# A hybrid decoder step on one core: the loads of the prompt's attention tiles move from SyncE's DMA queue to GpSimd's, with new times of issue

## The chip, the cores and the metric

The kernel runs on one core of a Trainium2 chip. Its time is the device time of one launch in microseconds (us), the median over runs. Engines are called as in the profile: PE is TensorE's matmul side and PEld its weight load, DVE is VectorE, ACT is ScalarE, POOL is GpSimd, SP is SyncE, which here does nothing but issue transfers. A "queue" of SP, ACT or POOL is the row of instructions of that engine: it runs in order, so an instruction that waits holds up all behind it.

## The reference, cut to what matters

One step of a two-layer decoder, for a prompt of 2048 new tokens and for 8 sequences of 8 new tokens each that continue 4096 cached tokens. The first layer is a gated linear recurrence, the second an attention with 16 heads of 64 over keys and values made once (`shared_kv`), with a cumulated log-forget value added to the scores. Cut to its core:

```
def fox_block(q, k, v, cq, ck, q_pos, k_pos):        # per block of queries, per head
    s = einsum('bqhd,bkhd->bhqk', q, k) * HEAD_DIM ** -0.5
    s = s + cq - ck                                   # cumulated log forget of query and key
    p = softmax(where(k_pos <= q_pos, s, -inf))
    return einsum('bhqk,bkhd->bqhd', p, v)

# prompt:  run_group(x_prompt, zero state, no past)          2048 tokens, causal
# samples: run_group(x_sample, state, past = cache[page_table])   8 x (4096 + 8) keys, 32 pages of 128 rows each
```

All numbers are float32; large products split an operand into a high and a low part of the type fp32r.

## The kernel before, in words

The program is written out by Python loops in program order, and a scheduler then places each instruction on its engine's queue by its own model of time; dependences become semaphore waits. The stages follow one another: the recurrence for a first and a second part of the prompt, the projections to keys, values, queries and gates (`phase_b`), the prompt's attention (`attention`), and the output projection (`project`). Beside the projections and the attention runs a second stream, the decoding of the 8 sequences (`decode`): SP fetches pages of cached keys and values (`pages`, L1093, four transfers of 256 KB into one `raw` tile, four such tiles), DVE transposes the key pages (`ktr`), PE makes scores (`dS`) and outputs (`dO`, L1262). `Side.along` sets how many steps of the one stream stand between two steps of the other, by hand-set costs.

The prompt's attention walks 64 units: 16 heads, each with four blocks of 512 queries (`qc` 0 to 3; even heads go up, odd heads down). A unit has 4(qc+1) ticks, one for each 128 keys, 40 ticks a head. In one tick PE multiplies keys and queries in two products (L1592 low and high parts `ka`, `qa`; L1593 `kbt`, `qbt`), ACT takes the exponential from a PSUM bank into a tile `p` (L1601; six of them, and the first tick of a unit goes into `acc`), and two ticks after every fourth, PE multiplies the four `p` with the values (`ops`, L1612) and POOL adds each `p` into `acc` (L108, `acc<-acc,p`), for the softmax's sum. A tile `p` comes free when both have read it. Ahead of a unit, PE makes its scores once more in part (`sx`, L1431) and DVE takes maxima.

Five kinds of tiles are loaded from scratch tensors in HBM for this:

- `qa` (L1419, `load_low`, 128 rows of 2 KB), one a unit, four buffers
- `qbt` (L1413, `load_unit`, 64 rows of 2 KB), one a unit, six buffers (`NQ`)
- `ka` (L1406, `load_head`, 128 rows of 8 KB), one a head, two buffers
- `kbt` (L1399 and L1400, `load_keys`, 64 rows of 8 KB and 3 rows of log-forget sums), one a head, two buffers
- `vvt` (L1407, in `load_head`, 512 KB in pieces of 256 bytes), one a head, two buffers

Those of head 0 (and the first units) go through ACT's queue. From then on `queue[0]` is SP, where they stand among the pages. `paged()` pins a transfer behind the latest page transfer in SP's queue. `done[1]` counts the units whose `qbt` was loaded, `done[2]` those whose scores are finished, and `LEAD` (18 ticks) says how far the maxima run ahead. After the unit's last product, its rows are scaled by the sums: small transfers `sums`, `r` and larger `sgt`, `ogd` go through SP too, and POOL does one multiplication for each (`sgt<-sgt,oT`).

Of the kernel before, what the change touches and what calls it, by code (L numbers as in the profile page):

```python
# [20 lines left out]
P = 128  # L21
# [6 lines left out]
H = 16  # L28
# [20 lines left out]
LEAD = 18  # L49
# [10 lines left out]
NQ = 6  # L60
AFT = 14
# [20 lines left out]
def f(ap):  # L82

    return ap.bitcast(F32)
# [3 lines left out]
def tile_hawk_fox(  # L88
# [8 lines left out]
    V, A, G, T, S = nc.vector, nc.scalar, nc.gpsimd, nc.tensor, nc.sync  # L97
# [9 lines left out]
    def tt(eng, out, a, b, op):  # L107
        eng.tensor_tensor(out, a, b, op=op)  # L108
# [8 lines left out]
    def paged():  # L117

        return tc.issue_after(place["S"]) if "S" in place else ExitStack()

    def together(mms, after=(), beside=False):

        first = mms[0]().ins
        for d in after:
            tc.add_manual_dep(first, d.ins.name, SYNC)
        if beside:
            behind("T", first)
        with tc.high_priority(), tc.issue_after(first):
            for mm in mms[1:]:
                mm()  # L130
# [38 lines left out]
    def dt_(name, shape):  # L169
        return dram.tile(shape, F32, name=name, tag=name)  # L170
# [11 lines left out]
    v_d = dt_("vd", [SEQ, D])  # L182
# [1151 lines left out]
    def attention(es):  # L1334
# [10 lines left out]
        vvs = [pool.tile([P, 16, HD], F32, name=f"vvt{i}") for i in range(2)]  # L1345
# [37 lines left out]
        units = [(h, qc) for h in range(H) for qc in ((0, 1, 2, 3) if h % 2 == 0 else (3, 2, 1, 0))]  # L1383
# [5 lines left out]
        def halves(h):  # L1389
            return ((0, half), (half, SEQ)) if h == 0 else ((0, SEQ),)  # L1390


        queue = [A]

        def load_keys(h):
            kb = kbs[h % 2]
            loaded.add(h)
            for lo, hi in halves(h):
                queue[0].dma_start(f(kb[0:64, lo:hi]), kd_d[h * HD:(h + 1) * HD, 1, lo:hi])  # L1399
                queue[0].dma_start(f(kb[64:67, lo:hi]), nc_d[h, :, lo:hi])  # L1400

        def load_head(h):
            hr = slice(h * HD, (h + 1) * HD)
            ka = pool.tile([P, SEQ], F32R, name="ka", tag="ka", bufs=2)
            for lo, hi in halves(h):
                queue[0].dma_start(f(ka[:, lo:hi]), kd_d[h * HD:(h + 1) * HD, :, lo:hi].rearrange("d x t -> (d x) t"))  # L1406
            queue[0].dma_start(vvs[h % 2][:, :, :], v_d[:, hr].rearrange("(k p) d -> p k d", p=P))  # L1407
            heads[h] = ka

        def load_unit(u):  # L1410
            h, qc = units[u]
            assert u < done[2] + NQ
            queue[0].dma_start(f(qbs[u % NQ][0:64, :]), qd_d[h * HD:(h + 1) * HD, 0, qc * 512:(qc + 1) * 512])  # L1413

        def load_low(u):
            if u < len(units):
                h, qc = units[u]
                qa = qas[u] = pool.tile([P, 512], F32R, name="qa", tag="qa", bufs=4)
                queue[0].dma_start(f(qa[:, :]), qd_d[h * HD:(h + 1) * HD, :, qc * 512:(qc + 1) * 512].rearrange("d x t -> (d x) t"))  # L1419
# [36 lines left out]
        def finish(u, ops, acc):  # L1456
            h, qc = units[u]
            pr, h2 = divmod(h, 2)
            if u % 8 == 0:
                oTs_["sums"] = pool.tile([P, 32], F32, name="sums", tag="sums", bufs=2)  # L1460
            sums = oTs_["sums"]
            if h2 == 0:
                oTs_[qc] = pool.tile([P, 512], F32, name="oT", tag="oT", bufs=5)
            oT = oTs_[qc][h2 * HD:(h2 + 1) * HD, :].rearrange("d (a r c) -> d a r c", a=2, r=2)
            for r in range(2):
                A.copy(oT[:, :, r, :], ops[r * HD:(r + 1) * HD, :].rearrange("d (a c) -> d a c", a=2))
            accs.append((qc, acc))
            if len(accs) == 4 or h == H - 1:
                later.after(2, lambda todo=accs[:]: total(h2, sums, todo, h >= H - 2))
                accs.clear()  # L1470
            if u >= len(units) - 4:
                later.after(5, lambda oT=[oTs_[qc]]: norm(pr, sums, qc, 1, oT))
            elif u % 8 == 7:
                later.after(5, lambda oT=[oTs_[c] for c in range(4)]: norm(pr, sums, 0, 4, oT))
# [53 lines left out]
        nks = [(qc + 1) * 4 for _, qc in units]  # L1528
        start = [sum(nks[:u]) for u in range(len(units))]
        done = [0, 0, 0]  # L1530
# [17 lines left out]
        tick = 0  # L1548
# [1 line left out]
        load_head(0)  # L1550
        load_low(0)
        load_low(1)
        queue[0] = S
        for _ in range(3):
            later.tick()
            yield 300
# [4 lines left out]
        def scores_bank():  # L1561

            if dec_done:
                wide[0] += 1
                if wide[0] % 2:
                    return psum["dec"].tile([P, 512], F32, name="st", tag="do"[wide[0] // 2 % 2], bufs=1)
            return ps3.tile([P, 512], F32, name="st", tag="st", bufs=2)
# [3 lines left out]
        def loads():  # L1571
            while lows[0] < len(units):
                v = lows[0]
                if tick < (start[v - 2] if v < 4 else min(max(start[v - 2], start[v - 3] + AFT), start[v] - 3)):
                    break
                with paged():
                    load_low(v)
                lows[0] += 1
            h, k = divmod(tick, 40)
            if k == 16 and h + 1 < H:  # L1580
                with paged():
                    load_head(h + 1)

        for u, (h, qc) in enumerate(units):
            for k in range(nks[u]):
                loads()
                ka, kb = heads[h], kbs[h % 2]
                qa, qb = qas[u], qbs[u % NQ]
                lo = max(0, k - qc * 4) * P
                ks = slice(k * P, (k + 1) * P)  # L1590
                ps = scores_bank()
                place["T"] = T.matmul(ps[:, lo:], ka[:, ks], qa[:, lo:], start=True, stop=False).ins  # L1592
                T.matmul(ps[:, lo:], kb[:, ks], qb[:, lo:], start=False, stop=(k < qc * 4))  # L1593
                if k >= qc * 4:
                    T.matmul(ps[:, lo:lo + P], identB[:, :], causal[:, :], start=False, stop=True)
                done[2] = u + (k == nks[u] - 1)
                if k == 0:
                    p = acc = pool.tile([P, 512], F32, name="acc", tag="acc", bufs=NACC)
                else:
                    p = pool.tile([P, 512], F32, name="p", tag="p", bufs=NP)  # L1600
                pair.append((k, lo, p, A.activation(p[:, lo:], ps[:, lo:], AF.Exp)))  # L1601

                def product(u=u, h=h, todo=pair, acc=acc, last=(k == nks[u] - 1)):


                    nonlocal ops
                    if todo[0][0] == 0:
                        ops = ops2[:, u % 2 * 256:u % 2 * 256 + 256]

                    def mm(k, lo, p, r):  # L1610
                        a0 = (lo // P + 1 - r) // 2
                        return T.matmul(ops[r * HD:(r + 1) * HD, a0 * P:], vvs[h % 2][:, k, :],  # L1612
                                        p[:, :].rearrange("p (a r c) -> p a r c", a=2, r=2)[:, a0:, r, :],
                                        start=(k == 0), stop=(last and k == todo[-1][0] - 1 + r))

                    together([partial(mm, k, lo, p, r) for k, lo, p, _ in todo for r in range(2) if lo <= (2 + r) * P],
                             [todo[-1][3]])
                    for k, lo, p, _ in todo:
                        if k:
                            tt(a_l(), acc[:, lo:], acc[:, lo:], p[:, lo:], ALU.add)  # L1620
                    if last:
                        finish(u, ops, acc)

                if k % 4 == 3:
                    later.after(2, product)
                    pair = []
                before = done[0]
                advance(tick)
                tick += 1
                later.tick()  # L1630
                if k + sum(nks[u - u % 4:u]) == 0 and h + 1 < H:
                    load_keys(h + 1)
                yield 4.1 * (512 - lo) * 0.42 + (done[0] - before) * 213

    lent, dec_done = {}, []
# [153 lines left out]
    done = 9  # L1789
# [6 lines left out]
    done = max(done, 41)  # L1796
# [61 lines left out]
    psum["att"] = banks(att, "psa", 6)  # L1858
    cost = sum(4.1 * 0.42 * (512 - max(0, k - qc * 4) * P) + 213 for qc in range(4) for k in range(4 * qc + 4)) * H
    side.along(attention(att), ((16 - FIRST) * TURN - side.spent) / (cost * SPAN))  # L1860
    place.clear()
    side.upto(1e12)
# [38 lines left out]
```

## Time and profile before

| | |
|---|---|
| median of 3 runs | 3025.98 us (3022.0 to 3029.27) |
| the profiled execution | 3028.43 us; its span, from first to last instruction, 3026.4 us |
| mean granted TensorE clock | 0.969 |
| busy share of the span | PE 93%, PEld 74%, DVE 60%, ACT 42%, POOL 36% |
| prompt's attention | from about 1740 to 2825 us of the span |
| bytes | 653.79 MB, 216 GB/s over the span |

Busy shares are averages over stages with different limits. A PE that is shown busy need not be at its peak, since the ends of pipelined matmuls are modelled, and instructions that issue transfers are not counted as busy on any engine.

### The profile page before, as it was taken

To read this page: it belongs to the slowest core of one execution; us is meant where nothing else is said; L and a number is where in the kernel's file an instruction comes from. 1 tells how busy PE (TensorE), PEld (TensorE's weight loads), DVE (VectorE), ACT (ScalarE), POOL (GpSimd) and SP (SyncE) were. 2 spreads that over 40 slices of the span, in tenths; PEclk is the share of its full clock that TensorE was granted. 3 is DMA by queue.
4 is the path that set the end of the run, shared out by engine and by line. 5 is a ranking of instruction groups with operands and counts; after the bars stand their busy time and mean duration, and the time that the engine had idled before them with its cause. 6 is when DMAs were issued, how large, how long until landed. Compare 5 with 4: busy or idle time off the path is not lost.

```text
span 3026.4 us, 60467 instructions
## 1 busy us (share of the span) xinstructions
PE 2803.4 (93%) x21614; PEld 2252.1 (74%) x21614; DVE 1805.5 (60%) x4012; ACT 1269.9 (42%) x2874; POOL 1084.4 (36%) x1199
## 2 busy tenths in 40 slices
PE   6998999998997999999999699998998999999998
PEld 5997789988887997888889556665665666565687
DVE  6877455425427775676564466656776756655344
ACT  4665342222125665534333234444544444355321
POOL 1653201000002653100000245665575656659422
PEclk9999999999998999999999889999999999999999
DMA  4224546888863226699999968898899888874343
GB/s 123 79 88 133 171 126 191 256 263 281 278 216 91 89 88 194 209 313 338 332 346 326 279 209 243 248 282 255 250 291 287 267 251 265 260 247 122 98 145 110
DMA packets 479103, 653.79 MB, mean 216 GB/s; under 512 B 91291, under 2 KB 277020, under 8 KB 471525
## 3 DMA queue, kind: packets, MB, share of 16 engines
q1 hardware_dynamic: 475174, 644.26, 67.4%
q10 hardware_dynamic: 3340, 3.56, 0.4%
q8 instruction: 171, 2.80, 0.4%
q0 software_dynamic: 288, 2.10, 0.2%
q14 instruction: 130, 1.06, 0.1%
HBM read 514.22 MB, written 135.16 MB: 215 GB/s over the span
## 4 chain that ended last, share of the span: by engine, by line
PE 59%; DMA 16%; DVE 9%; ACT 6%; SPq 5%; issue 3%; POOL 1%; ACTq 0%; DVEq 0%; POOLq 0%
PE ops L1612 7%; PE st L1592 4%; PE y L383 4%; PE y L384 4%; PE y L385 4%; DMA raw<-in_cache_k_dram 4%; PE sx L1431 4%; PE dO L1262 3%; DMA raw<-in_cache_v_dram 3%; PE st L1593 3%; PE dS L1148 3%; PE kv L383 3%; PE kv L385 3%; PE kv L384 3%; SPq L1093 2%
## 5 line engine op out<-in xcount | busy, mean ns | idle before, releaser
L108 POOL TENSOR_TENSOR acc<-acc,p 128x512 f32<-128x512 f32 (+3 forms) x576 | 640.9, 1114 | 347.7 <-PE ops L1612 211.2
L1601 ACT ACTIVATE p<-st 128x512 f32<-128x512 f32 (+3 forms) x576 | 291.3, 525 | 400.1 <-PE st L1593 177.5
L1180 DVE STREAM_TRANSPOSE ktr<-raw 128x1024 f32<-128x1024 f32 x256 | 308.2, 1226 | 125.1 <-DMA raw<-in_cache_k_dram 116.5
L1433 DVE TENSOR_REDUCE mxs<-sx 128x1 f32<-128x512 f32 x384 | 255.0, 681 | 141.0 <-PE sx L1431 139.6
L383 PE MATMUL kv<-wh,xh 128*128 128x256 f32 (+3 forms) x1088 | 310.0, 288 | 6.4 <-ACT wh L427 4.7
L384 PE MATMUL kv<-wl,xh 128*128 128x256 f32 (+3 forms) x1088 | 309.3, 287 | 5.7 <-DVE wl L428 5.7
L385 PE MATMUL kv<-wh,xl 128*128 128x256 f32 (+3 forms) x1088 | 309.6, 286 | 2.7 <-DMA xl<-xld 2.7
L1592 PE MATMUL st<-qa,ka 128*128 128x512 f32 (+3 forms) x640 | 269.9, 422 | 13.3 <-ACT p L1601 7.5
L1612 PE MATMUL ops<-p,vvt 128*64 128x256 f32 (+1 forms) x2176 | 262.9, 369 | 1.0 <-ACT p L1601 0.7
L1431 PE MATMUL sx<-kbt,qbt 96*128 96x512 f32 (+3 forms) x640 | 229.2, 416 | 29.9 <-DMA qbt<-qd 24.2
L1113 POOL TENSOR_TENSOR qw<-qb,amask 128x128 f32<-128x128 f32 x64 | 29.1, 460 | 618.1 <-PE dS L1148 325.3
L428 DVE SCALAR_TENSOR_TENSOR wl<-wst,gv,wh 128x256 fp32r<-128x256 f32 (+1 forms) x384 | 169.4, 504 | 131.8 <-ACT wh L427 131.5
L427 ACT ACTIVATE wh<-wst,gv 128x256 fp32r<-128x256 f32 (+1 forms) x384 | 164.6, 499 | 190.2 <-DMA wst<-in_w_kv_dram 72.7
L1593 PE MATMUL st<-qbt,kbt 128*128 128x512 f32 (+3 forms) x640 | 236.9, 370 | 0.0
L383 PE MATMUL qg<-xh,wh 128*128 128x512 f32 (+2 forms) x640 | 229.4, 359 | 0.0
L384 PE MATMUL qg<-xl,wh 128*128 128x512 f32 (+2 forms) x640 | 228.2, 357 | 0.0
L385 PE MATMUL qg<-xh,wl 128*128 128x512 f32 (+2 forms) x640 | 227.5, 356 | 0.6 <-DVE wl L428 0.6
L1612 PEld LDWEIGHTS ops<-p,vvt 128*64 128x64 f32 x2176 | 161.5, 141 | 88.2 <-issue 19.8
L383 PEld LDWEIGHTS kv<-wh,xh 128*128 128x128 f32 (+1 forms) x1088 | 203.5, 188 | 13.2 <-ACT wh L427 6.8
L384 PEld LDWEIGHTS kv<-wl,xh 128*128 128x128 f32 (+1 forms) x1088 | 203.2, 188 | 10.1 <-DVE wl L428 6.9
L385 PEld LDWEIGHTS kv<-wh,xl 128*128 128x128 f32 (+1 forms) x1088 | 204.8, 188 | 7.0 <-issue 3.7
L1592 PEld LDWEIGHTS st<-qa,ka 128*128 128x128 f32 x640 | 123.7, 193 | 112.8 <-issue 54.4
(297 smaller groups left out, 6356.3 us busy)
## 6 DMA issues: line engine op xcount, KB each, us to landing
raw<-in_cache_k_dram SPq DMA_DIRECT2D x512, 256.0 KB
raw<-in_cache_v_dram SPq DMA_DIRECT2D x512, 256.0 KB
wst<-in_w_kv_dram SPq DMA_DIRECT2D x48, 512.0 KB
wst<-in_b_w_in_dram SPq DMA_DIRECT2D x48, 512.0 KB
xt<-in_x_prompt_dram SPq DMA_DIRECT2D x32, 512.0 KB
wst<-in_a_w_in_dram SPq DMA_DIRECT2D x64, 256.0 KB
out_dram<-kf SPq DMA_DIRECT2D x128, 128.0 KB
sc<-cd SPq DMA_DIRECT2D x16, 1024.0 KB
```

What stands on the lines that cost most here:

```text
L108: eng.tensor_tensor(out, a, b, op=op)
L383: T.matmul(ps, lh(k), rh(k), start=(k == 0), stop=False)
L384: T.matmul(ps, lh(k), rl(k), start=False, stop=False)
L385: T.matmul(ps, ll(k), rh(k), start=False, stop=(k == nk - 1))
L428: V.scalar_tensor_tensor(wl[:, k, :], st[:, k, :], gk, f(wh[:, k, :]), op0=ALU.mult, op1=ALU.subtract)
L1180: behind("V", V.transpose(t.kts[pp][:, n], raw[:, :, pp * 256:(pp + 1) * 256]).ins)
L1431: T.matmul(ps[:, :w], qb[0:96, j * P:(j + 1) * P], kb[0:96, ck * 512:ck * 512 + w], start=True, stop=True)
L1433: place["V"] = V.reduce_max(mx[:, j, ck:ck + 1], ps[:, :w], axis=AX.X).ins
L1592: place["T"] = T.matmul(ps[:, lo:], ka[:, ks], qa[:, lo:], start=True, stop=False).ins
L1593: T.matmul(ps[:, lo:], kb[:, ks], qb[:, lo:], start=False, stop=(k < qc * 4))
L1601: pair.append((k, lo, p, A.activation(p[:, lo:], ps[:, lo:], AF.Exp)))
L1612: return T.matmul(ops[r * HD:(r + 1) * HD, a0 * P:], vvs[h % 2][:, k, :], p[:, :].rearrange("p (a r c) -> p a r c", a=2, r=2)[:, a0:, r, : ...
```

## The change

The loads of `qa`, `qbt`, `ka` and `kbt` after the first head's go through POOL's queue and are no longer pinned to the pages; `vvt` stays in SP's queue, pinned to a page. The times of issue in program order are new: `load_low` two ticks after the start of the unit three before (at most four buffers are in use); `load_unit` by a loop of its own, as soon as a buffer is free and the unit starts within `LEAD + nks/2 + 7` ticks; `load_keys` for the next head at tick 3 of a head (it was tick 0, behind that tick's products) and `load_head` at tick 12 (it was 16). No arithmetic changes.

```
         def load_head(h): ...
-            queue[0].dma_start(vvs[h % 2][:, :, :], v_d[:, hr].rearrange("(k p) d -> p k d", p=P))
+            with paged() if h else ExitStack():
+                (S if h else queue[0]).dma_start(vvs[h % 2][:, :, :], v_d[:, hr].rearrange("(k p) d -> p k d", p=P))
...
-        queue[0] = S
+        queue[0] = G
...
         def loads():
             while lows[0] < len(units):
                 v = lows[0]
-                if tick < (start[v - 2] if v < 4 else min(max(start[v - 2], start[v - 3] + AFT), start[v] - 3)):
+                if tick < (start[v - 2] if v < 4 else start[v - 3] + 2):
                     break
-                with paged():
-                    load_low(v)
+                load_low(v)
                 lows[0] += 1
+            while done[1] < len(units) and done[1] < done[2] + NQ and tick >= start[done[1]] - LEAD - nks[done[1]] // 2 - 7:
+                load_unit(done[1])
+                done[1] += 1
             h, k = divmod(tick, 40)
-            if k == 16 and h + 1 < H:
-                with paged():
-                    load_head(h + 1)
+            if k == 3 and h + 1 < H:
+                load_keys(h + 1)
+            if k == 12 and h + 1 < H:
+                load_head(h + 1)
...
-                if k + sum(nks[u - u % 4:u]) == 0 and h + 1 < H:
-                    load_keys(h + 1)
```

Where the instructions come to stand is shown at three places. The line numbers behind the change are higher by one to four (`qa` L1420, `qbt` L1414, `vvt` L1408). First SP's queue between two pages, where the tiles of head 2 are loaded, before:

```order
L1093 DMA raw<-in_cache_k_dram 128x512
L1419 DMA qa<-qd 128x512
L1399 DMA kbt_19862<-kd 64x2048
L1400 DMA kbt_19862<-ncd 3x2048
L1406 DMA ka<-kd 128x2048
L1407 DMA vvt_19859<-vd 128x16x64
L1413 DMA qbt_19866<-qd 64x512
```

and the same place of SP's queue after the change:

```order
L1093 DMA raw<-in_cache_k_dram 128x512
L1408 DMA vvt_19859<-vd 128x16x64
L1086 TENSOR_LOAD pt_115
L1093 ISA
L1093 DMA raw<-in_cache_v_dram 128x512
```

Five of six loads between these two pages are gone from SP; `vvt` stays. Second, POOL's queue at the end of head 0's longest unit and the start of head 1's (`qw` and `gmx` belong to the decoding), before:

```order
L108 TENSOR_TENSOR acc<-acc,p 128x512 x2
L108 TENSOR_TENSOR acc<-acc,p 128x384
L1113 TENSOR_TENSOR qw<-qb,amask 128x128 x2
L108 TENSOR_TENSOR acc<-acc,p 128x256
L108 TENSOR_TENSOR acc<-acc,p 128x128
L1128 MEMSET gmx 128x8
L108 TENSOR_TENSOR acc<-acc,p 128x512 x12
```

and after, with the loads for head 2 and the units to come:

```order
L1113 TENSOR_TENSOR qw<-qb,amask 128x128
L1420 DMA qa<-qd 128x512
L1406 DMA ka<-kd 128x2048
L1399 DMA kbt_19862<-kd 64x2048
L1400 DMA kbt_19862<-ncd 3x2048
L1414 DMA qbt_19866<-qd 64x512
L108 TENSOR_TENSOR acc<-acc,p 128x128
L1128 MEMSET gmx 128x8
L108 TENSOR_TENSOR acc<-acc,p 128x512 x12
```

Five loads in a row stand between the unit's last two additions, ahead of twelve full additions. Third, POOL's queue at the last change of heads with loads (from head 13 to head 14), before:

```order
L108 TENSOR_TENSOR acc<-acc,p 128x128
L108 TENSOR_TENSOR acc<-acc,p 128x512 x4
L108 TENSOR_TENSOR acc<-acc,p 128x384
L108 TENSOR_TENSOR sgt<-sgt,oT 128x512
L108 TENSOR_TENSOR acc<-acc,p 128x256
```

and after:

```order
L108 TENSOR_TENSOR acc<-acc,p 128x128
L108 TENSOR_TENSOR acc<-acc,p 128x512 x2
L1420 DMA qa<-qd 128x512
L1414 DMA qbt_19863<-qd 64x512
L108 TENSOR_TENSOR acc<-acc,p 128x512
L1420 DMA qa<-qd 128x512
L1406 DMA ka<-kd 128x2048
L1399 DMA kbt_19870<-kd 64x2048
L1400 DMA kbt_19870<-ncd 3x2048
L1414 DMA qbt_19864<-qd 64x512
L108 TENSOR_TENSOR sgt<-sgt,oT 128x512
```

Seven loads stand among the additions here, and six more follow further on (`qa`, `qbt`, `qa`, `qbt`, `qa`, `qa`): 13 in all around and behind this change of heads. PE's queue holds the same instructions before and after, with the decoding's products beside the same units; only some `sx` stand a few ticks earlier or later.

## Prediction

> **What bounds the kernel now.** I read the page first, then the busy times by stretch, then who waited for whom on PE, ACT and SP within the prompt's attention, and last the timeline at single waits. The page's busy shares:
>
> ```profile
> span 3026.4 us, 60467 instructions
> PE 2803.4 (93%) x21614; PEld 2252.1 (74%) x21614; DVE 1805.5 (60%) x4012; ACT 1269.9 (42%) x2874; POOL 1084.4 (36%) x1199
> ```
>
> PE is the bound over the whole program, and POOL's 36% is an average that hides where its work lies. The change touches only the attention, so I split it where the decoding ends (the first row: its last page is fetched at 2702 us), and add the stretch in which the attention starts:
>
> ```profile
> L1093 SPq DMA_DIRECT2D raw<-in_cache_v_dram x316: 327/333/8803, 1780.4 to 2702.1; - x158
> ...
> core 0: us, PE busy (x) PEld busy (x) DVE busy (x) ACT busy (x) POOL busy (x), PEclk, DMA share, GB/s
> 1730.00:1758.00 28.00, 14.23 (x51) 7.87 (x51) 7.78 (x26) 3.17 (x10) 0.67 (x2) 0.50 0.79 211
> 1760.00:2720.00 960.00, 903.58 (x8240) 578.11 (x8239) 626.72 (x1328) 436.70 (x1080) 589.64 (x562) 0.97 0.84 259
> 2720.00:2820.00 100.00, 94.22 (x560) 58.44 (x558) 52.26 (x99) 57.99 (x121) 90.68 (x77) 1.00 0.38 109
> ```
>
> Of POOL's 1084 us, 590 + 91 lie in these two stretches. In the body (960 us, decoding beside it) PE is busy 94% and POOL 61%; 56 us of PE are idle, all that a better supply could win. In the tail (the last two heads, no decoding) POOL is busy 91%: there it is as near to the bound as PE. What PE's idle time in the body waited for, and ACT for POOL in both stretches (the second ACT row is the tail's):
>
> ```profile
> PE dO L1262 <- DMA raw<-in_cache_v_dram: 19.4, 13, 3.1
> PE rp L1505 <- DMA r<-rs: 11.3, 5, 4.2
> PE st L1592 <- ACT p L1601: 5.9, 17, 0.8
> ...
> ACT p L1601 <- PE st L1593: 177.4, 124, 6.0
> ...
> ACT p L1601 <- POOL acc L108: 16.6, 10, 3.5
> ...
> ACT p L1601 <- POOL acc L108: 21.5, 24, 2.0
> ```
>
> No row shows PE waiting for `qa`, `qbt`, `ka` or `kbt` in the body: the loads that move are in time already. What they may cost today is what stands behind them on SP. In the body ACT waits for POOL to free a `p` 10 times only; in the tail, a tenth as long, 24 times.
>
> **What leaves SP.** SP's queue in the body, waits of the prompt's loads:
>
> ```profile
> SPq L1413 <- PE st L1595: 20.7, 9, 5.3
> ...
> SPq L1399 <- PE sx L1431: 16.5, 2, 16.0
> ...
> SPq L1419 <- PE st L1595: 14.4, 3, 8.7
> SPq L1413 <- PE sx L1431: 13.7, 13, 6.1
> ```
>
> These 65 us hold back pages, and so do the transfers. One case:
>
> ```profile
> 1782.80 0.43 SPq L1406 DMA_DIRECT2D ka<-kd  x1
> 1783.27 0.43 SPq L1407 DMA_DIRECT2D vvt<-vd  x1
> 1784.33 8.18 SPq L1093 DMA_DIRECT2D raw<-in_cache_k_dram  x4
> ...
> 1793.60 1.92 SPq L1093 DMA_DIRECT2D raw<-in_cache_v_dram  x4
> ...
> 1800.79 1.07 PE L1262 MATMUL dO<-raw,sx 128*32 128x256 f32 x16 [2.18 <-DMA raw<-in_cache_v_dram]
> ```
>
> After `ka` (1 MB) and `vvt` (512 KB) the next four page issues take 8.18 us instead of about 2, and PE waits 2.18 us for a value page. But `vvt`, the one in small pieces, stays on SP, and the bytes stay the same. So I take about half of the 19.4 us as won, 10 us, and of the 11.3 us for `r` (a small transfer issued behind pages and loads, of which the pages stay) 3 us: **−13 us**. The bounds are 0 and −31 us.
>
> [...] No row here shows two queues side by side in the body. [...]
>
> **What POOL gets.** Counts and durations of the moved issues, and the only transfer that POOL issues before:
>
> ```profile
> L1419 SPq DMA_DIRECT2D qa<-qd x62: 319/430/7628, 1739.8 to 2772.4; - x62
> ...
> L1413 SPq DMA_DIRECT2D qbt<-qd x61: 444/464/6912, 1728.6 to 2736.5; - x61
> ...
> L1399 SPq DMA_DIRECT2D kbt<-kd x15: 444/473/1372, 1729.1 to 2720.8; - x15
> ...
> L1400 SPq DMA_DIRECT2D kbt<-ncd x15: 293/482/502, 1737.8 to 2721.5; - x15
> ...
> L1406 SPq DMA_DIRECT2D ka<-kd x15: 331/430/1694, 1782.8 to 2723.5; - x15
> ...
> L324 POOL DMA_INDIRECT lg<-in_cache_logf_dram,idx x2: 1058/1140/1223, 465.8 to 486.3; - x2
> ...
> 1696.80 1.81 POOL L1354 MEMSET kbt<- 64x2048 f32 x1 [0.33 <-DMA raw<-in_cache_k_dram]
> ```
>
> 62+61+15+15+15 = 168 issues. A plain transfer issued by POOL is in no row. The nearest is the indirect one, 1.06 to 1.22 us of POOL for 128 rows of 8 KB, the shape of `ka`. I take its 1.14 us for each; the ends are SP's median, 0.43 us, and, as the longest that POOL spends on a tile of this size, the clearing of `kbt`, 1.8 us. Behind each issue in POOL's queue stand additions into `acc`; for these waits ACT (a `p` comes free only when POOL has read it), and for ACT waits PE's next scores.
>
> Waits on POOL for a free buffer I cost at nothing: the issue stands among additions whose `p` was made some ticks after the last read of that buffer, so POOL gets there later than PE. If that cover is gone, SP's 65 us above are the price, now in front of the additions.
>
> *Tail.* Around and behind the last change of heads stand 13 issues: 13 × 1.14 = 15 us. POOL has 100 − 90.7 = 9.3 us of idle there; since part of it is forced by order (the start of a unit waits for its first product) I let half absorb: **+10 us** (bounds: 13 × 0.43 = 5.6 less 9.3, no loss; 13 × 1.8 = 23).
>
> *Body.* 155 × 1.14 = 177 us come to 590 of 960: POOL goes from 61% to 80%. Whether that costs is a question of crowding: five loads in a row are 5.7 us in front of a run of additions. I scale ACT's wait for POOL as in a queue, by busy over idle: from 0.61/0.39 = 1.6 to 0.80/0.20 = 4.0, so 16.6 us become 42, 25 more. How much of it reaches PE? Of the 16.6 us now, PE shows 5.9 us of waiting for `p`, a third; with PE already busy 94%, I take half: **+12 us** (bounds: at 0.43 us an issue 68%, 2.2/1.6 of 16.6, 6 more, a third of them 2; at 1.8 us 90%, 9 / 1.6 of 16.6 = 95, 78 more, all of them).
>
> **The start.** The first scores wait, while all loads of head 0 come through ACT's queue:
>
> ```profile
> PE sx L1431 <- DMA qbt<-qd: 24.2, 1, 24.2
> PE st L1592 <- DMA qa<-qd: 4.3, 1, 4.3
> ```
>
> The transfers are busy 79% in that stretch at 211 GB/s. POOL is free at 1730 us (0.67 us of work in 28) and would now issue `ka` of head 1 (1 MB) there, which SP issued at 1782.8. 1 MB at 211 GB/s is 5 us of the transfer engines; I let **+3 us** of it fall on head 0's loads, bounds −3 (SP's own loads gone from between the pages) and +5.
>
> **Sum.** −13 + 10 + 12 + 3 = +12 us. The profiled execution took 3028.43 us (span 3026.4), 2.4 above the median of 3025.98; 12 us on the median give **3038 us**. The bounds added up: −31 + 0 + 2 − 3 = −32, and 0 + 23 + 78 + 5 = +106. What is late next where the page wait goes: PE's next instruction there needs `p` from ACT, which is the wait that grows.
>
> **Rivals.**
>
> *Faster: the pages come free and POOL has room.* For: POOL is idle 39% of the body, ACT waits there ten times longer for PE's scores than for POOL (177.4 and 16.6 us), and the page wait shown above follows a `ka`. If an issue costs POOL no more than SP (0.43 us) and all waits for value pages and `r` go: −31 + 0 + 2 + 3 = −26, 3000 us; with two thirds of the waits, −21 + 2 + 2 = −17, 3009. It decides when an issue on POOL is below about 0.8 us. Against: the only row for such an issue says 1.06 or more, and `vvt` stays. 0.28, at about 3009 us.
>
> *No relief of transfers.* The wait for pages stays as it is since bytes, transfer engines and `vvt` stay: 0 + 10 + 12 + 3 = +25, 3051 us. Against it speaks that 8.18 us of issue followed `ka` and `vvt` together. [...] 0.14.
>
> *POOL becomes the bound.* If an issue holds POOL 1.8 us, or waits for buffers: body 155 × 1.8 = 279, 90% busy, half of 78 = +39; tail 23 − 5 = +18; +3, −13: +47, 3073 us. For: additions come in runs, in which POOL has no idle time as in the tail. Against: the clearing writes 64 partitions and an issue writes none. 0.13.
>
> *The change doesn't do what it says:* the loads get stuck behind additions and PE starts waiting for `qa` or `kbt`. They are issued ten ticks or more ahead of use, and 40 ticks take about 68 us (960 us for some 14 heads), so POOL would have to be 17 us behind. Five such waits of 3 us on the forecast: 3053 us. 0.03.
>
> **How the numbers follow.** The forecast has 0.42, with an own range of 3026 to 3056 us. Range for 8 in 10: from 3003 (most of the faster case) to 3078 (the bound case at its middle). A measurement of this kernel can tell 0.2%, 6 us, from no change. Faster by more: most of the 0.28 and the forecast's low edge, 0.29. Within: 0.14, from the forecast's lower part and weak gains. Slower: the rest of the forecast and the three slow rivals, 0.57.
>
> **What would show it.** In the changed kernel's profile: the duration of POOL's issues (right at 1.0 to 1.25 us); POOL busy, with issues, about 80% of the body; ACT's wait for POOL, 42 us in the body for 16.6; PE's wait for value pages about 10 us for 19.4; the last two heads 10 us longer. The forecast is wrong if issues cost POOL under 0.6 us, if ACT's wait for POOL does not grow, or if PE waits for `qa`, `qbt`, `ka` or `kbt`.

## The result, and the profile after

The changed kernel takes 3104.13 us (3095.34 to 3110.5), the kernel before, run beside it, 3024.66: a ratio of 1.0259 (95% interval 1.0225 to 1.0293), which is 78 us of 3025. The forecast was 3038 us, its range 3003 to 3078. The direction was right, the size far too small. One run of e10_gate (3550.91 us) and one of e18_pin (5326.34 us), far slower than their others, are left out of what follows. The profiled execution took 3095.34 us; its page begins:

```profile
span 3093.4 us, 60582 instructions
PE 2823.9 (91%) x21614; PEld 2257.0 (73%) x21614; DVE 1807.8 (58%) x4012; ACT 1271.0 (41%) x2874; POOL 1166.7 (38%) x1367
```

POOL has 82 us more, where 168 issues at the 1.14 us assumed make 192. (Other than is said ahead of the prediction, POOL's issues do count as busy: it has 1367 instructions for 1199, 168 more.) Busy times by stretch, cut where head 14's first exponential begins and where head 15's last ends, two rows of before and two of after (time, then PE, PEld, DVE, ACT and POOL busy, granted clock, DMA share, GB/s):

```profile
1757.00:2721.60 964.60, 908.18 (x8260) 581.52 (x8258) 630.76 (x1337) 439.09 (x1087) 591.16 (x563) 0.97 0.83 258
2721.60:2825.00 103.40, 96.81 (x577) 59.75 (x576) 52.23 (x96) 61.36 (x129) 93.93 (x79) 1.00 0.39 112
...
1758.00:2764.10 1006.10, 920.20 (x8253) 583.97 (x8253) 632.50 (x1331) 438.16 (x1082) 666.95 (x712) 0.95 0.81 246
2764.10:2895.00 130.90, 110.63 (x602) 66.39 (x601) 54.98 (x105) 62.80 (x134) 98.48 (x93) 0.90 0.32 90
```

The attention took 1068.0 us and now takes 1137.0; outside it 2 us came back, which leaves the 67 us between the spans. The body lost 41.5 us, the last two heads 27.5. In both PE's *busy* time grew too: 908.2 to 920.2 and 96.8 to 110.6, together 25.8 us, while the granted clock fell from 0.97 to 0.95 and from 1.00 to 0.90. Not all of this is slower products: 22 products of the output projection fall into the second stretch for 4 before, some 7 us. Over the whole program the same 21614 products take 2823.9 us for 2803.4, 20.5 us more. The other 43.2 us are PE idle time (56.4 to 85.9, and 6.6 to 20.3). What it waited for in the body (us in total, times, longest), and whom ACT and POOL waited for:

```profile
ACT p L1605 <- POOL acc L108: 42.1, 20, 11.1
POOL sgt L108 <- DMA sgt<-sgd: 41.4, 7, 13.8
POOL qa L1420 <- PE st L1597: 32.6, 2, 32.3
POOL qa L1420 <- PE st L1599: 32.3, 20, 9.9
...
DVE ktr L1180 <- DMA raw<-in_cache_k_dram: 25.5, 9, 6.8
...
PE st L1596 <- ACT p L1605: 19.9, 23, 9.2
...
PE rp L1506 <- DMA r<-rs: 14.3, 5, 7.9
...
PE sx L1432 <- DVE mxs L1436: 8.5, 3, 7.8
...
PE dS L1148 <- DVE ktr L1180: 7.9, 2, 7.5
...
PE dO L1262 <- DMA raw<-in_cache_v_dram: 7.0, 6, 2.1
```

POOL's wait of 32.3 us for `qa` is at the start, where POOL waited as long before (33.0 us, for the first value products). The last column is what is new. In the body of before no wait of PE lasted longer than 4.2 us (for `r`); now four different ones last 7.5 to 9.2 us. The longest, in the timeline (start, duration, engine, line, and in brackets the idle time before it and what ended it):

```profile
2618.65 0.43 SPq L1522 DMA_DIRECT2D sgt<-sgd  x1
2618.90 0.53 POOL L1414 DMA_DIRECT2D qbt<-qd  x1
...
2633.23 1.26 POOL L108 TENSOR_TENSOR sgt<-sgt,oT 128x512 f32<-128x512 f32 x1 [13.81 <-DMA sgt<-sgd]
2634.45 3.71 POOL L108 TENSOR_TENSOR acc<-acc,p 128x128 f32<-128x128 f32 x6
2634.93 0.60 ACT L1605 ACTIVATE p<-st 128x512 f32<-128x512 f32 x1 [11.05 <-POOL acc L108]
...
2635.58 0.80 PE L1596 MATMUL st<-qa,ka 128*128 128x512 f32 x1 [9.18 <-ACT p L1605]
```

SP asks for `sgt` at 2618.65; it lands 14.6 us later. POOL waits for it with six additions behind, so all six `p` are held, ACT stops, PE stops. At the same place of before, `sgt` was asked for at 2583.80, its multiplication ran at 2591.96 after a wait of 5.16, and no addition stood ready behind it. What the clock does around this wait (PE busy, granted clock, DMA share, GB/s):

```profile
2616.00:2624.00 8.00, 6.52 (x49) 1.00 1.06 368
2624.00:2628.00 4.00, 2.41 (x64) 1.00 0.99 226
2628.00:2632.00 4.00, 0.00 (x0) 0.62 0.79 218
2632.00:2640.00 8.00, 4.42 (x42) 0.50 0.03 6
2640.00:2644.00 4.00, 4.00 (x18) 0.67 0.90 277
```

The clock falls to 0.50 in the wait and is still there some 6 us after PE has work again: by windows of 1 us it is 0.50 from 2629 to 2642 us and 1.00 from 2643. This wait is so paid twice: a product of `st` (L1597, 128x512) takes 0.63 us behind it at 0.50, and took 0.39 ahead of it at 1.00. Shorter ones can be, too: in the kernel before, PE waited 2.08 us for a page up to 1924.24 us and 2.88 us for `r` up to 2481.61 us, and the clock stood at 0.50 from 1926 to 1928 and from 2482 to 2488 us. Its rows around them:

```profile
1920.00:1940.00 20.00, 17.45 (x217) 0.91 0.81 260
...
2480.00:2500.00 20.00, 18.39 (x103) 0.83 0.74 247
```

By windows of 2 us the attention of before has 12 stretches at a lowered clock, that of the changed kernel 18, the longest 22 us for 10.

In the last two heads the timeline shows another stop (ACT's casts of the output weights, L101, stand ahead of the exponentials):

```profile
2779.19 1.05 ACT L101 CAST woh<-wst 128x1024 fp32r<-128x1024 f32 x1 [10.25 <-DMA wst<-in_b_w_out_dram]
2780.14 0.59 ACT L1605 ACTIVATE acc<-st 128x512 f32<-128x512 f32 x1
...
2780.79 0.80 PE L1596 MATMUL st<-qa,ka 128*128 128x512 f32 x1 [6.50 <-ACT acc L1605]
```

`ka`, `kbt` and `qbt` left POOL at 2764.1 to 2765.7, in the middle of SP's loads of those weights. The price of an issue on POOL (by line: ns, least, median, most):

```profile
L1420 POOL DMA_DIRECT2D qa<-qd x62: 553/572/631, 1724.6 to 2841.0; - x62
L1414 POOL DMA_DIRECT2D qbt<-qd x61: 528/528/583, 1725.3 to 2801.6; - x61
L1406 POOL DMA_DIRECT2D ka<-kd x15: 541/541/577, 1728.0 to 2764.1; - x15
```

It is half of the 1.14 us assumed, from 128 KB (`qbt`, 0.528) to 1 MB (`ka`, 0.541). By the prediction's own list this price should have brought the faster case. So the price of an issue does not explain the loss.

### The profile page after: what moved, and what is told of

The parts are those of the page before. It is cut to its first block, busy times and chain, and to the rows that moved or that the text cites. A ratio compares the mean times of both kernels' runs of the same rounds, so it can differ in the third digit from the quotient of the medians.

```text
span 3093.4 us, 60582 instructions
## 1 busy us (share of the span) xinstructions
PE 2823.9 (91%) x21614; PEld 2257.0 (73%) x21614; DVE 1807.8 (58%) x4012; ACT 1271.0 (41%) x2874; POOL 1166.7 (38%) x1367
## 4 chain that ended last, share of the span: by engine, by line
PE 48%; DMA 19%; DVE 6%; SPq 4%; ACT 4%; issue 3%; POOL 1%; DVEq 0%; ACTq 0%; POOLq 0%
PE ops L1616 6%; DMA raw<-in_cache_k_dram 5%; PE st L1596 3%; PE sx L1432 3%; DMA raw<-in_cache_v_dram 3%; PE dO L1262 3%; PE y L383 3%; PE y L384 3%; PE y L385 3%; PE kv L383 3%; PE kv L385 3%; PE dS L1148 3%; PE kv L384 3%; PE st L1597 2%; SPq L1093 2%
## 5 line engine op out<-in xcount | busy, mean ns | idle before, releaser
L1596 PE MATMUL st<-qa,ka 128*128 128x512 f32 (+3 forms) x640 | 272.5, 426 | 41.7 <-ACT p L1605 20.3
L1597 PE MATMUL st<-qbt,kbt 128*128 128x512 f32 (+3 forms) x640 | 239.0, 373 | 0.0
L383 PEld LDWEIGHTS kv<-wh,xh 128*128 128x128 f32 (+1 forms) x1088 | 204.8, 189 | 12.4 <-ACT wh L427 6.3
```

What stands on the lines that cost most here:

```text
L383: T.matmul(ps, lh(k), rh(k), start=(k == 0), stop=False)
```

## Experiments

Ratios are to the kernel before, run beside each; 0.01 is 30 us. Three theories to begin with. *Two queues*: the bytes of POOL's queue share the transfer engines with SP's (in the body SP's packets take 65.1% of the 16 engines' time and POOL's 15.0%, where SP's took 82.8% before), so `sgt`, `r`, pages and weights land late. *New times*: the loads come in bunches and too early. *POOL's time*: issues, and waits for buffers, stand in front of additions.

**Times alone, queue alone.** e1_times changes one line of the changed kernel; e2_queue takes the kernel before with its times:

```
e1_times:  -  queue[0] = G      e2_queue:  -  queue[0] = S
           +  queue[0] = S                 +  queue[0] = G      (loads unpinned; vvt on S, pinned)
```

> The changed kernel with its new times of issue, but the moved loads in SyncE's queue again (not pinned to a page). Theory 'two queues' (POOL's transfers run beside SP's and share the transfer engines with them, so that sgt, the last weights and pages land late): the loss goes, 3015 to 3045 us. Theory 'new times' (the loads come in bunches and too early): the loss stays, 3085 to 3115 us. Theory 'POOL's time' (155 issues of 0.55 us in front of additions): 3015 to 3045 us as well.

> The kernel before with its old times of issue, but the loads of qa, qbt, ka and kbt in GpSimd's queue, unpinned, and vvt on SyncE pinned, as in the change. 'Two queues': 3080 to 3120 us, as the changed kernel. 'New times': 3015 to 3045 us. 'POOL's time': 3080 to 3120 us.

e1_times: 1.0025 (1.0002 to 1.0047). e2_queue: 1.0243 (1.0222 to 1.0264). The new times cost some 8 us; the queue makes the loss, with the old times as well. *New times* falls.

**The late `sgt`.** e4_sgtV lets VectorE multiply, e10_gate puts five ticks more between the request for it and its use, e16_gate_before makes the same edit to the kernel before:

```
e4_sgtV:   -  tt(G, sg, sg, oT[qc - q0], ALU.mult)     +  tt(V, sg, sg, oT[qc - q0], ALU.mult)
e10_gate, e16_gate_before:
           -  later.after(3, gate)                     +  later.after(8 if n == 4 else 3, gate)
           -  (AFT + 7) * (qc // 2)                    +  (AFT + 12) * (qc // 2)
```

> The changed kernel with the multiplication sgt<-sgt,oT on VectorE in place of GpSimd, so that POOL no longer waits for the transfer of sgt in front of its additions (41 us of waits in 7 places in the changed kernel, up to 13.8 us, of which 9 us each reached PE twice). Theory 'POOL held by a late transfer': 20 to 40 us come back, 3065 to 3085 us. If the stall only moves to VectorE, which then holds maxima and transposes: 3095 to 3115 us. 'POOL's time': at most 10 us come back.

> The changed kernel with five ticks (about 8 us) more between the fetch of sgt and its use, and between the two pairs of fetches, for all but the last heads; nothing else moves. If sgt landing late (41 us of waits in 7 places) starts the stalls at the changes of even heads: 15 to 40 us come back, 3065 to 3090 us. If it only shares the crowding with its neighbours (r, key pages): 3090 to 3112 us.

> The kernel before with five ticks more between the fetch of sgt and its use, and between the two pairs of fetches (the edit of e10_gate). Its waits for sgt are 27.5 us on POOL in 8 places, at most 7.4 us, and PE waits 11.5 us for r. If POOL's wait reaches PE only when it is longer than the six tiles p cover, nothing is won: 3018 to 3032 us. If waits of any length cost, 10 us or more are won: 3005 to 3016 us.

e4_sgtV: 1.0235 (1.0213 to 1.0257), nearly the whole loss. In its waits in the attention (us in total, times, longest), DVE now stands for `sgt`, and PE 28.1 us for DVE's maxima (1.3 in the same row of before):

```profile
DVE sgt L108 <- DMA sgt<-sgd: 45.5, 9, 10.6
PE sx L1432 <- DVE mxs L1434: 28.1, 18, 6.8
```

e10_gate: 1.0189 (1.0144 to 1.0234); about 20 us came back. The late `sgt` is a part, not the root. e16_gate_before: 1.0062 (1.004 to 1.0083), slower, a miss of both expectations: PE's wait for value pages rose from 19.4 to 27.2 us. So the five ticks are no gain in themselves.

**The last two heads.** e11_tail goes back to SP's queue from tick 30 of head 13:

```
 def loads():
+    queue[0] = G if tick < 40 * 13 + 30 else S
```

> The changed kernel with GpSimd's queue until tick 30 of head 13, and SyncE's queue from there on. It asks for the last two heads, which took 131 us (from the first exponential of head 14 to the last of head 15) for 103.5 before. If POOL's transfers of that stage hold up the last weights' (ACT waited 10.3 us for them): the stage takes 103 to 112 us, the kernel 3078 to 3090 us. If the stage is late for another reason: 122 us or more, 3095 to 3112 us.

1.0153 (1.0118 to 1.0188), 3074.01 us. Its last two heads in the busy times by stretch:

```profile
2765.80:2870.20 104.40, 98.84 (x583) 61.09 (x582) 53.05 (x101) 62.68 (x133) 93.62 (x80) 0.98 0.39 113
```

104.4 us for 130.9, at a clock of 0.98, with the body as slow as before this edit (1004.7). So POOL's loads from there on cost this stage some 27 us, and the whole kernel 30.

**Issues alone.** e3_issue adds 168 transfers of 64 bytes to POOL in the kernel before; e13_pinned adds 163, each queued behind the latest addition:

```
e3_issue:    +  G.dma_start(tiny[r:r + 1, c * 16:c * 16 + 16], kd_d[0:1, 0, 0:16])
e13_pinned:  +  with tc.issue_after(place["G"]):
             +      G.dma_start(tiny[r:r + 1, c * 16:c * 16 + 16], kd_d[0:1, 0, 0:16])
```

> The kernel before with 168 transfers of 64 bytes added to GpSimd's queue at the changed kernel's places, which nobody reads; the loads themselves stay with SyncE. It asks what the issues alone cost POOL and the kernel. 'POOL's time': 92 us more on POOL, the kernel 30 us or more slower, 3055 us up. 'Two queues' and 'new times': 64 bytes take no bandwidth and wait for no buffer, so 0 to +12 us, 3020 to 3038 us.

> The kernel before with about 160 transfers of 64 bytes added to GpSimd's queue at the changed kernel's times, which nobody reads, each now queued behind the latest addition into acc so that none is pulled ahead. The loads stay with SyncE. If the issues alone (0.5 us each, 80 us of POOL) make the loss: 3070 us or more. If they have room in POOL's idle time: 3020 to 3045 us.

e3_issue: 1.0291 (1.0254 to 1.0328). It does not test what it should: nothing held the transfers at their places, and all 168 were issued before head 1 had begun, up to thirteen at a time. From its timeline of POOL:

```profile
1842.67 5.78 POOL L1575 DMA_DIRECT2D tiny<-kd  x12
1848.47 1.69 POOL L108 TENSOR_TENSOR acc<-acc,p 128x128 f32<-128x128 f32 x2
1850.10 1.96 POOL L1575 DMA_DIRECT2D tiny<-kd  x4
```

The three longer units of head 0 lost 81 us there. e13_pinned: 1.0058 (1.004 to 1.0077), some 18 us, for 82.8 us of POOL. Its group of issues (count, busy us, mean ns, idle time) and its busy times by stretch, body and last two heads:

```profile
L1576 POOL DMA_DIRECT2D tiny<-kd x163 | 82.8, 511 | 2.7 <-issue 2.7
...
1752.00:2708.60 956.60, 899.32 (x8255) 577.28 (x8255) 632.47 (x1336) 438.23 (x1087) 662.31 (x713) 0.97 0.84 261
2708.60:2824.30 115.70, 101.48 (x578) 61.15 (x577) 49.92 (x96) 60.59 (x129) 96.95 (x92) 0.96 0.35 105
```

This execution took 3027.92 us, the fastest of seven, 15 us under their median. In it the body lost nothing with POOL at 662 us (the changed kernel: 667), and the last two heads 12 us. ACT did wait longer for POOL than before, though never as long at once as in the changed kernel (whole attention; before, e13_pinned, changed kernel):

```profile
ACT p L1601 <- POOL acc L108: 38.1, 34, 3.5
...
ACT p L1617 <- POOL acc L1636: 56.0, 44, 5.2
...
ACT p L1605 <- POOL acc L108: 67.6, 46, 11.1
```

Little of it reached PE, whose wait for `p` in the scores was 7.5, 11.5 and 20.3 us.

**Half of the loads; another queue.** e7_q leaves `qa`, `qbt` on POOL, e8_k `ka`, `kbt`; e6_act sends all through ScalarE's queue:

```
e7_q:    ka, kbt:  +  (S if queue[0] is G else queue[0]).dma_start(...)
e8_k:    qa, qbt:  +  (S if queue[0] is G else queue[0]).dma_start(...)
e6_act:            -  queue[0] = G       +  queue[0] = A
```

> The changed kernel with only qa and qbt (123 issues, 24 MB, rows of 2 KB) in GpSimd's queue; ka, kbt go through SyncE's, unpinned. 'POOL's time': three quarters of the issues and all waits for buffers stay, so 3085 to 3105 us. 'Two queues' by bytes: half the loss, 3055 to 3080 us; if it is the 1.5 MB burst at each change of heads in rows of 8 KB that delays sgt: nearly no loss, 3030 to 3050 us.

> The other half: only ka and kbt (45 issues, 24 MB, rows of 8 KB, 1.5 MB at once per head) in GpSimd's queue; qa, qbt go through SyncE's, unpinned. 'POOL's time': a quarter of the issues, 3035 to 3055 us. 'Two queues' by bytes: half the loss, 3055 to 3080 us; if it is the burst in rows of 8 KB: nearly the whole loss, 3080 to 3105 us.

> The changed kernel with the moved loads in ScalarE's queue: a queue beside SP's still, but no instruction on POOL. 'Two queues': the loss stays, 3080 to 3120 us. 'POOL's time': it goes, 3015 to 3050 us (168 issues of about 0.45 us on ACT, which is busy 45% of this stage, and some waits for buffers in ACT's queue).

e7_q: 1.0061 (1.0038 to 1.0085). e8_k: 1.0082 (1.0057 to 1.0107). They add up to some 43 us, all loads cost 78: neither *POOL's time*, which put three quarters on `qa` and `qbt`, nor an even split by bytes. e6_act: 1.019 (1.0163 to 1.0218). It says little: ACT's own queue now stops ahead of exponentials, and PE waits 61.7 us for `p` in its value products. Its waits in the attention:

```profile
PE ops L1616 <- ACT p L1605: 61.7, 25, 9.4
ACT p L1605 <- DMA rawn<-ksd: 19.9, 2, 10.6
ACT p L1605 <- DMA raw<-in_cache_k_dram: 17.8, 5, 6.5
```

**Loads cut between the queues.** e5_row lets POOL fetch the first row of each load and SP the others; e9_rows16 does so with 16 rows (one of the three of log-forget sums); e12_spfirst exchanges the two queues:

```
+  G.dma_start(to[:n], src[:n])      # e5_row: n = 1; e9_rows16: n = 16
+  S.dma_start(to[n:], src[n:])      # e12_spfirst: S first, G the rest
```

> The changed kernel with every moved load cut in two: GpSimd's queue fetches only its first row (2 or 8 KB), SyncE's queue all other rows, unpinned. POOL so keeps every issue at its place with the same waits for buffers, and the bytes go back to SP's queue. Theory 'two queues' (it is the bytes beside SP's queue that make sgt, weights and pages late): 3025 to 3055 us. Theory 'POOL's time' (92 us of issues and 65 us of waits for buffers in front of additions): 3085 to 3115 us.

> The run with a row cut off again, now in sixteenths: GpSimd's queue fetches the first 16 rows of each moved load (of the log-forget sums, one of three), SyncE's queue the rest, so that no transfer has 127 rows. POOL keeps every issue at its place with its waits for buffers; 75 to 88% of the bytes, and the waits for buffers too, are in SP's queue again. 'POOL's time': 3085 to 3115 us. 'Two queues' (bytes beside SP's queue) and 'SP not held' (nothing in SP's queue waits for PE's scores any more, pages run ahead and sgt stands behind a longer backlog): 3030 to 3060 us.

> The same cut the other way: SyncE's queue fetches the first 16 rows of each moved load, GpSimd's the rest. SP's queue is held by the same waits for buffers again, but most bytes still run beside it. 'Two queues' by bytes: 3080 to 3115 us. 'SP not held': 3030 to 3060 us. 'POOL's time': 3085 to 3115 us.

e5_row: 1.3423 (1.3391 to 1.3455), no answer: the transfers of 127 or 63 rows hold up SP's queue. There an issue of `qbt` (63 rows) lasts 3.63 us in the median and up to 40.5, for 0.46 in the kernel before, one of `kbt` (63 rows) 5.25 for 0.47, and one of `qa` (127 rows) up to 39.6 us. From 1757 to 2900 us all transfers together moved 130 GB/s, and PE waited up to 62.4 us for a page. From its waits:

```profile
PE dO L1262 <- DMA raw<-in_cache_v_dram: 394.8, 20, 62.4
```

Why such issues last so long, no run shows. e9_rows16: 1.0288 (1.0243 to 1.0333), the whole loss, with most bytes in SP's queue again. e12_spfirst: 1.0379 (1.0339 to 1.0418), slower than any theory expected. Both double the number of transfers. They speak against *two queues*, and against the idea that SP's queue only has to be held by PE again.

**Bytes or queue.** e14_few_pool cuts the loads after the first heads' to 16 rows (the others keep older contents), with POOL's order kept (its waits for `qa` behind the start are 22.5 us for 32.5); e15_few_sync does the same through SP:

```
+  n = to.shape[0] if full else min(16, to.shape[0])
+  queue[0].dma_start(to[:n], src[:n])       # e14_few_pool: G, e15_few_sync: S
```

> The changed kernel with each moved load cut to its first 16 rows (all rows for the first two heads' keys and the first units' queries; the other rows keep older contents, so the attention is computed from partly stale keys and queries). POOL keeps every issue at its place with its waits; some 40 of 50 MB are not moved at all. If POOL's issues and waits make the loss: 3075 us or more, far above the control e15_few_sync. If the bytes beside SP's queue make it: near the control, within 20 us.

> The control of e14_few_pool: the same few rows with the same times of issue, through SyncE's queue (the attention computed from partly stale keys and queries as there). 40 MB less at about 260 GB/s leave the transfer engines some 150 us more idle: 2995 to 3035 us by every theory.

e14_few_pool: 1.0107 (1.0073 to 1.0142), 3058.73 us. e15_few_sync: 0.9937 (0.9915 to 0.9959), 3006.79. The first misses both expectations: it is under 3075 us, and not near its control. So POOL's queue costs 52 us over SP's with few bytes, and 71 with all (3104.13 less e1_times' 3033.31). If the parts add up, that leaves some 19 us for the bytes beside SP's queue, with an uncertainty nearly as large (the intervals of the four times are 7 to 11 us to either side). *Two queues* falls as the main cause.

**The place on POOL.** 163 issues cost 18 us, 168 loads with few bytes 52. In e13_pinned each stands behind an addition; in the changed kernel the scheduler places the loads, and behind the start 12 times four or five stand in a row. e18_pin pins all moved loads, e20_pin_qa `qa` alone:

```
+  with tc.issue_after(place["G"]) if queue[0] is G and "G" in place else ExitStack():
+      queue[0].dma_start(to, src)           # place["G"]: the latest addition into acc
```

> The changed kernel with each moved load queued on POOL behind the latest addition into acc at its time of issue (as the loads stood pinned behind pages before). Same queue, same bytes, same count of issues. If the loss is the place of the loads on POOL (pulled ahead, in rows, waiting for buffers with additions behind them: 67 us of such waits from the start of the attention): they become rare and 25 to 50 us come back, 3050 to 3080 us. If it is the bytes beside SP's queue, or the issues: 3090 to 3115 us.

> The changed kernel with only qa queued on POOL behind the latest addition; qbt, ka and kbt stay where the scheduler puts them, ten times four in a row in front of additions. If POOL's waits for qa's buffer (32 us behind the start, in 21 places, up to 9.9 us), with a row of loads and additions behind them, make the part that e18_pin took back: 3050 to 3072 us. If the rows themselves make it: 3085 to 3110 us.

e18_pin: 1.0094 (1.0063 to 1.0125), 3056.39 us: 48 us came back with the same queue, bytes and count. At the last change of heads, where seven loads stood around one addition, POOL's queue now reads:

```
L1397 DMA qa<-qd 128x512
L1397 DMA kbt_19870<-kd 64x2048
L1397 DMA kbt_19870<-ncd 3x2048
L1628 TENSOR_TENSOR acc<-acc,p 128x256
L1628 TENSOR_TENSOR acc<-acc,p 128x512
L1628 TENSOR_TENSOR acc<-acc,p 128x128
L1397 DMA qa<-qd 128x512
L1628 TENSOR_TENSOR acc<-acc,p 128x512 x2
L1397 DMA ka<-kd 128x2048
L1628 TENSOR_TENSOR acc<-acc,p 128x512
```

Behind the start no row is longer than three, and at one load only, a `ka`, does POOL wait (1.9 us, for ACT). Its body and last two heads by stretch, and its only wait of a load on POOL:

```profile
1760.00:2739.90 979.90, 913.30 (x8255) 584.03 (x8253) 633.25 (x1330) 438.11 (x1081) 671.06 (x713) 0.96 0.83 254
2739.90:2856.30 116.40, 105.84 (x597) 63.80 (x598) 50.14 (x104) 61.72 (x133) 98.51 (x95) 0.97 0.34 101
...
POOL ka L1397 <- ACT p L1609: 1.9, 1, 1.9
```

e20_pin_qa: 1.0137 (1.0101 to 1.0172), 3070.05 us, between the two. It did not part the waits from the rows as meant: the waits went over to `qbt`, 28.6 us of them behind the start as `qa` had 32.5, though none longer than 4.8 us for 9.9. POOL's waits behind the start:

```profile
POOL qbt L1418 <- PE st L1603: 28.6, 20, 4.8
```

So it is shown that the place of the loads in POOL's queue makes the larger part of the loss. Whether a long wait for a buffer or the row of loads behind it weighs more stays open, and so does what part the other engines' order, which the scheduler also moves, has in it. Two earlier runs bear on the first question. e7_q has more of such waits behind the start than the changed kernel (up to 11.0 us at once), but rows of at most two loads, and loses 18 us:

```profile
POOL qa L1420 <- PE st L1599: 29.8, 21, 4.8
...
POOL qa L1420 <- PE st L1597: 18.3, 3, 11.0
```

e3_issue has rows of up to thirteen, all within one head, with no tile of PE's to wait for and next to no bytes, and loses 88 us where e13_pinned's nearly equal count loses 18. Both speak for the rows; neither is a clean test, since e7_q also leaves `ka` and `kbt` to SP. No run had more `p` tiles, which would test ACT's cover. None of the versions that load all rows beats the kernel before.

## Why the prediction was wrong, step by step

- **Pages, −13: the size was met, the reason is not shown.** PE's wait for value pages fell from 19.4 to 7.0 us, −12.4 for the −10 taken; the wait for `r` did not fall by 3 but rose by 3.0. Pages may have come earlier, or PE, held up elsewhere for 29.5 us more in the body, may have come later.
- **The price of an issue: wrong.** 0.53 to 0.57 us, near SP's end of the bounds, 92 us in all for 192.
- **ACT's wait for POOL, 42 us: met by luck.** 42.1 us, and PE's wait for `p` rose by 14.0 for the 12 forecast. But POOL is 66% busy, not 80%, where my queue rule gives (0.66/0.34)/(0.61/0.39) of 16.6 = 21 us. Two single waits for `sgt` (10.4 and 13.8 us) held ACT for 9.3 and 11.1 us; they are 20 of the 25 us more. The crowding that I reckoned with is there, but by itself it hardly reaches PE: with as much work on POOL, e13_pinned's ACT waits 56.0 us for POOL in the whole attention for 38.1 before, and PE 11.5 us for `p` for 7.5.
- **The step that failed: waits in POOL's queue "cost at nothing".** The issue was to stand where POOL gets later than PE; instead POOL waited 32.3 us in 20 places behind the start for `qa`'s buffer, up to 9.9 us at once. I asked only when a buffer comes free, and not what the scheduler does with the order of everything else on POOL: loads in rows of five that wait for PE with additions behind them, and additions that now stand behind the wait for `sgt`. e18_pin, in which both the rows and these waits are gone, puts 48 of the 78 us there; the waits alone, in e7_q, were not that dear. POOL's queue as the change's section prints it showed a row of five loads at both of its places; I priced them at their issue time.
- **The tail, +10: near the issues' cost by luck, the rest was missing.** e13_pinned's issues cost 12 us there, at half the price assumed: by my sum 13 × 0.55 us less half of 9.3 would have been 2. The stage lost 27.5 us. SP's loads of the last weights came to stand beside POOL's loads, and ACT, which I had not looked at, waited 10.25 us for them with exponentials behind. Of the 27.5 us, 13.7 are PE's idle time; of the 13.8 us more of products, some 10 are 25 products that fall into this stretch only now, an estimate from their durations before, and about 4 are slower products.
- **The clock: missing.** 20.5 of the 67 us between the spans are the same products taking longer, with the mean granted clock at 0.956 for 0.969. No term had it, although the kernel before already had stretches at 0.50 behind waits of 2 to 3 us.
- **The start, +3:** 1.1 us (first exponential at 1757.4 and 1758.5).
- **The rivals.** "POOL becomes the bound" named a price (1.8 us) that was wrong and a wait (for buffers) that did come; its 3073 us is nearest. "No relief of transfers" forecast an unchanged page wait, which fell; with e14_few_pool, the bytes are not the main matter either. PE's waits for the moved tiles, a sign of being wrong, did not come: behind the start there is none.

## What to carry to other kernels

Price a transfer on a computing engine's queue by what stands behind it there, not by its issue time alone: here 82.8 us of issues cost some 18 us (e13_pinned), and another place of the same loads on POOL took back 48 of 78 us (e18_pin). Look for a wait in that queue with ready work behind, and count how many tiles cover it. Where a scheduler places instructions, a pin that seems to be about one queue (here behind a page) also keeps loads from gathering in rows (behind the start 12 times four or five without pins, never more than three with e18_pin's); give a moved load a new pin on its new engine. And look at the granted clock behind PE's waits: here a wait of 9.2 us, and before also waits of 2 to 3 us, cost slower products behind them, at a clock of 0.50, besides their own length.

## What the runs showed of the hardware

A plain transfer took 0.52 to 0.57 us of POOL's time in the median of each of the five moved kinds (24 KB: 0.52; 1 MB: 0.54), and 0.51 in the mean for 64 bytes (e13_pinned), against medians of 0.43 to 0.48 on SP in the kernel before. Transfers cut to 127 or 63 rows made the kernel 34% slower, where cuts at sixteen rows did not (e9_rows16: 2.9%, e12_spfirst: 3.8%). The granted clock stood at 0.50 from 2770 to 2788 us of the changed kernel, although PE had work for 6.9 of the last 8 us of it. In the kernel before it fell to 0.50 behind PE waits of 2.08 and 2.88 us.
